# Modulation units of the latent attention layers in halves, spread over query tiles and gates

## The chip, the cores and the metric

The kernel runs as one program on one core of a Trainium2 chip. The metric is the device time of one execution in microseconds (us). All engine times below come from one profiled execution.

## The reference, cut to what matters

Four trunk layers run one after the other on 512 latent tokens and 256 context tokens, both 1024 wide. Layers 0 and 3 mix tokens with latent attention, layer 1 with a windowed attention, layer 2 with a long convolution. Each layer is modulated by two conditions (one for the latent tokens, one for the context):

```python
mx = cond_x @ w_mod[layer] + b_mod[layer]          # (1, 1024) @ (1024, 3072)
shift_x, scale_x, gate_x = jnp.split(mx[:, None, :], 3, axis=-1)
hx = rmsnorm(x, g_pre[layer]) * (1.0 + scale_x) + shift_x
...
x = x + gate_x * rmsnorm(yx, g_post[layer])
```

So `w_mod` of a layer, 12 MB, is read for two rows of conditions. The shift and scale of a layer are wanted when its input is normed; its gate is wanted when its output is added to the stream. A latent attention layer projects the normed input to a key and value latent with the rotary key (320 columns), a query latent (512 columns) and a gate (1024 columns), and goes on to heads, attention and the output projection.

## The kernel before, in words

**Modulation units.** A unit is 512 of the 3072 columns of one layer's modulation, read as four blocks of 512 KB (`want_mod`). For each block `mod_chunk` issues four narrow matmuls (line 442; each shows as two records in the trace, so a block is 8 records and a unit 32). A unit of shift or scale (`mod_ab_unit`) then copies the finished bank to a buffer `m` (ScalarE, line 455), turns it by four transposes (line 459), and reduces it on VectorE (lines 463 to 469). A gate unit (`mod_g_unit`) copies into a buffer that is held until the end of the layer (line 480) and adds the bias row by a small DMA (line 481). `fill` runs one whole unit through; units wait in the list `fillers`.

**Two streams of weights.** `Stream.take` hands out the next block and asks for later ones: `W` for the layer's own weights, `M` for modulation blocks. All loads go through SyncE's queue (line 211, or 209 for some), in one order. `cap_d` and `look_d` bound how many blocks of a stream are loaded and how far ahead. `W` blocks are split into two parts on ScalarE and VectorE (lines 230 to 237) and leave their buffer then; a modulation block leaves its buffer when its matmuls are done.

**Buffers.** All loaded blocks, `m`, the held gate buffer, the normed tile of a query or key tile (`cn`) and the ring of rotary temporaries come out of one arena of float32 buffers of 1024 words a partition. In a latent attention layer the gate and output tensor `og` takes 6144 words of 13760, so that seven such buffers are left. `slot` gives the free buffer that was freed longest ago, and a load into it has to wait for the last reader of what was there.

**The stage that the change touches** is the first part of `layer_A`. It has three loops: six token tiles of the key and value latent (24 matmuls of 320 columns each), six token tiles of the query latent in layer 0 and four in layer 3 (24 matmuls of 512 columns), and eight gate chunks (24 matmuls of 512 columns, in layer 0 also 24 of 256). Each latent tile is normed: a square on ScalarE (line 704), two small GpSimd operations (358, 359), a scaling on VectorE (707), transposes (710) and a split (341, 342). A gate is finished by ScalarE and VectorE (347, 348). Matmuls of latent tiles stand at lines 577 to 579, those of gates at line 588. Tile results are in two double banks `pb`; gates, transposes and modulation go round four banks `pa`.

**Where the units stand.** In layer 0 there are six units (four of shift and scale of layer 1, two of the gate of layer 0). A whole unit goes ahead of each of the key and value tiles 3, 4 and 5 and of the query tiles 0, 1 and 2. In layer 3 there are two units (its own gate), ahead of the key and value tiles 4 and 5. From the first of these tiles on, `M` may hold two blocks (`MC`).

**Order.** The order of the instructions on each engine is planned while the program is built (`TileContext` with `schedule_with_timeline_sim=True`), from the order of the source and from modelled times. On the chip each engine follows that order. So a unit's matmuls can stand inside the matmuls of another tile.

Of the kernel before, what the change touches and what calls it, by code (L numbers as in the profile page):

```python
# [15 lines left out]
AF = mybir.ActivationFunctionType  # L16
# [4 lines left out]
D = 1024  # L21
# [7 lines left out]
AH = 2  # L29
SU = 2  # L30
WX = {25: (3, 2), 27: (3, 2), 29: (3, 3)}
UKS = (3, 4)
UQ = 0
UC = 0
MC = 2
CH = ((0, 384),)
LS = 2
WD = 3
# [97 lines left out]
class Ring:  # L136
# [6 lines left out]
    def next(self):  # L143
        self.i += 1
        return self.blocks[self.i % len(self.blocks)]
# [125 lines left out]
class Kern:  # L271
# [138 lines left out]
    def want_mod(self, unit):  # L410
        kind, L, c = unit
        w = self.io["w_mod"][L].rearrange("(k p) n -> p k n", p=P)
        if kind == "g":
            c += 4
        for kb in range(4):
            n0, k0 = 512 * c + 256 * (kb // 2), 4 * (kb % 2)
            self.M.want(("mod", L, c, kb), w[:, k0:k0 + 4, n0:n0 + 256], split=False)
# [27 lines left out]
            if kb < 3:  # L445
                yield

    def mod_ab_unit(self, L, c, bank=None):

        nc = self.nc  # L450
        bank = bank or self.a
        ps = bank()
        yield from self.mod_chunk(L, c, ps)
        m = self.fs(512)
        nc.scalar.activation(m.ap, ps, AF.Copy)
        yield
        ps = bank()
        for b in range(4):
            nc.tensor.transpose(ps[:, P * b:P * b + P], m.ap[:, P * b:P * b + P], self.ident)
        m.free()  # L460
        part, k0 = c // 2, 4 * (c % 2)
        r = self.col(8).rearrange("p (b s) -> p b s", b=4)
        nc.vector.tensor_reduce(r, ps.rearrange("p (b j s) -> p b s j", b=4, j=4)[:, :, 0:2, :], axis=AX.X, op=ALU.add)
        bm = self.bmod[:, L, 4 * c:4 * c + 4, None].to_broadcast([P, 4, 2])
        if part == 0:
            nc.vector.tensor_tensor(self.ab[:, L, 1, k0:k0 + 4], r, bm, op=ALU.add)
        else:
            nc.vector.scalar_tensor_tensor(r, r, 1.0, bm, op0=ALU.add, op1=ALU.add)
            nc.vector.tensor_tensor(self.ab[:, L, 0, k0:k0 + 4], r, self.gpre[:, L, k0:k0 + 4, None].to_broadcast([P, 4, 2]),
                                    op=ALU.mult)  # L470

    def mod_g_unit(self, L, c, bank=None):

        nc, io = self.nc, self.io
        ps = (bank or self.a)()
        yield from self.mod_chunk(L, 4 + c, ps)
        if c == 0:
            self.mg[L] = self.fs(D)
        m = self.mg[L].ap[:, 512 * c:512 * c + 512]
        nc.scalar.activation(m, ps, AF.Copy)  # L480
        nc.sync.dma_start(out=m[2:3, :], in_=io["b_mod"][L:L + 1, 2048 + 512 * c:2560 + 512 * c])
        yield

# [12 lines left out]
        m.free()  # L496
        return g

    def unit(self, bank=None):
        kind, L, c = self.fillers.pop(0)  # L500
        return (self.mod_ab_unit if kind == "ab" else self.mod_g_unit)(L, c, bank)

    def fill(self, n=1):
        for _ in range(n):
# [186 lines left out]
    def layer_A(self, L, j, h, ctx_out, last):  # L691
        nc, R, F = self.nc, self.R, self.F
# [8 lines left out]
        def normed(ps, n, dst, t):  # L701

            ssq = self.col()
            nc.scalar.activation(self.trash[:, 0:n], ps, AF.Square, accum_out=ssq)
            self.rstd(ssq, n)
            cn = self.fs(n)
            nc.vector.tensor_scalar(cn.ap, ps, ssq, None, op0=ALU.mult)
            pt = self.a()
            for k in range(n // P):
                nc.tensor.transpose(pt[:, P * k:P * k + P], cn.ap[:, P * k:P * k + P], self.ident)  # L710
            cn.free()
            self.split_ps(dst[:, 0, :, P * t:P * t + P], dst[:, 1, :, P * t:P * t + P],
                          pt[:, 0:n].rearrange("p (k n) -> p k n", n=P))

        UK = UKS[0 if ctx_out else 1]
        units = sum(f[:2] in (("ab", L + 1), ("g", L)) for f in self.fillers)

        wide = Banks(self.halves())
        ckv = self.rl(2 * 2 * T)
# [6 lines left out]
        self.W.pump(4, 3)  # L726
        wk = lambda k: (ws[k // 2][1][0][:, k % 2], ws[k // 2][1][1][:, k % 2])
        for t in order:
            if t == UK:
                self.M.cap_d = self.M.look_d = MC  # L730
            if units and t >= UK:
                self.fill()
                units -= 1
            ps = wide.next()
            self.mm_tok(ps[:, 0:320], h, t, wk, 320)
            normed(ps[:, 0:256], 256, ckvv, t)
            ks = small.next()
            kv4 = ks.v(2, 2, 64)
            if t < 4:
                kf = self.ropes.next()  # L740
                self.rope_ps(kf.v(1, 64), ps[:, 256:320].rearrange("p (a b) -> p a b", a=1), t, 1)
                src = kf.ap[:, 0:64]
            else:
                kf = None
                src = ps[:, 256:320]
            nc.scalar.activation(kv4[:, 0], src[:, None, :].to_broadcast([P, 2, 64]), AF.Copy)
            nc.vector.tensor_tensor(kv4[:, 1], src[:, None, :].to_broadcast([P, 2, 64]), kv4[:, 0].bitcast(F32), op=ALU.subtract)
            pt = self.a()
            for i in range(2):
                nc.tensor.transpose(pt[:, P * i:P * i + P], ks.ap[:, P * i:P * i + P].bitcast(F32), self.ident)  # L750
            nc.vector.tensor_copy(krv[:, :, P * t:P * t + P], pt[:, 0:256].rearrange("p (a b) -> p a b", a=2))
# [4 lines left out]
        cqv = cq.v(2, 4, TQ)  # L756
        ws = [self.W.take(("cq", k)) for k in range(0, KD, 2)]
        for t in (order if ctx_out else qt):
            if units and t >= UQ:
                self.fill()  # L760
                units -= 1
            ps = wide.next()
            self.mm_tok(ps, h, t, wk, 512)
            normed(ps, 512, cqv, t)
# [2 lines left out]

        spans = [(0, NX), (NX, NC)] if ctx_out else [(0, NX)]
        for c in range(8):
            if units and c >= UC:  # L770
                self.fill()
                units -= 1
            blk, (wh, wl) = self.W.take(("gate", c))
            outs = [self.a()[:, 0:n] for _, n in spans]
            self.mm_ch(outs, lambda part, k, i: self.h_at(h, part, k, *spans[i]), lambda k: (wh[:, k], wl[:, k]))
            blk.free()
            for (t0, n), o in zip(spans, outs):
                self.gate2(ogv[:, c, t0:t0 + n], o)
        for b in h:
            b.free()  # L780
        self.lo_pool = True
        self.M.cap_d = self.M.look_d = 1

# [152 lines left out]
        units = [(hd, t) for hd in range(8) for t in qt]  # L936
# [861 lines left out]
```

## Time and profile before

| What | Value |
|---|---|
| median of 3 runs | 1950.54 us (1945.15 to 1960.34) |
| time of the profiled execution | 1953.32 us |
| span of its instructions | 1951.5 us |
| granted TensorE clock, mean | 0.984 of full speed |
| TensorE (PE) busy | 1820.0 us, 93% of the span |
| VectorE (DVE), ScalarE (ACT), GpSimd (POOL) busy | 1182.5, 812.3, 521.6 us |

PE is the matmul unit and PEld its weight loads, which lie beside matmuls. SPq is SyncE's queue, which issues DMAs. In a table of stretches the clock is given as a part of full speed; 0.50 is 1.2 GHz and 1.00 is 2.4 GHz. The profiled execution is 2.8 us above the median of the runs.

### The profile page before, as it was taken

The numbers are of one execution on the slowest core, as the hardware profiler recorded it, in microseconds if no ns is written. First come the engines' busy times: TensorE is split into PE (matmuls) and PEld (weight loads), VectorE is DVE, ScalarE is ACT, GpSimd is POOL, SyncE is SP. The second block draws the span as 40 slices with busy tenths as digits, with TensorE's granted clock in tenths as the row PEclk, the third lists the DMA queues.
The fourth block names the chain that finished last, engine by engine and source line by source line (L and its number), as shares of the span: only waits on it lengthen the run. The fifth ranks groups of instructions, "written<-read, shape, count | busy, mean of one in ns | idle before, by whom it ended". The sixth has DMA issues, their size and how long they took to land.

```text
span 1951.5 us, 30304 instructions
## 1 busy us (share of the span) xinstructions
PE 1820.0 (93%) x11628; PEld 1576.6 (81%) x11628; DVE 1182.5 (61%) x2364; ACT 812.3 (42%) x1686; POOL 521.6 (27%) x523
## 2 busy tenths in 40 slices
PE   5879799999999899999989899999998998999998
PEld 3557588999988888888868699999987777889986
DVE  6684134787755367676675445566668553477663
ACT  3473132555544255565664422222222343354451
POOL 5561000000213321221231344444445221000120
PEclk9999899999999999999999999999999999999999
DMA  7857521001133112222362622222221335310121
GB/s 214 259 175 226 158 78 31 22 24 43 44 109 117 57 48 83 76 67 67 99 223 103 204 60 85 70 74 76 76 77 60 122 120 154 87 33 23 44 76 54
DMA packets 186356, 186.31 MB, mean 95 GB/s; under 512 B 16600, under 2 KB 164952, under 8 KB 186212
## 3 DMA queue, kind: packets, MB, share of 16 engines
q1 hardware_dynamic: 186212, 184.39, 30.6%
q8 instruction: 91, 1.49, 0.3%
q14 instruction: 53, 0.43, 0.1%
HBM read 160.24 MB, written 24.12 MB: 94 GB/s over the span
## 4 chain that ended last, share of the span: by engine, by line
PE 77%; DVE 10%; DMA 6%; ACT 3%; issue 3%; POOL 1%; SPq 0%; POOLq 0%; DVEq 0%; ACTq 0%
PE pb L588 13%; PE pb L622 11%; PE pa L588 10%; PE pb L873 5%; PE pa L912 4%; PE pa L1068 3%; PE pa L1049 3%; DMA arena_f<-in_w_mod_dram 3%; PE pa L1525 2%; PE pa L1558 2%; PE pa L442 2%; PE pa L898 2%; PE pa L1177 2%; PE pb L577 2%; PE pb L578 2%
## 5 line engine op out<-in xcount | busy, mean ns | idle before, releaser
L588 PE MATMUL pb<-arena_r 128*128 128x512 f32 (+1 forms) x1536 | 293.2, 345 | 8.1 <-DVE arena_f L1498 3.6
L588 PEld LDWEIGHTS pb<-arena_r 128*128 128x128 f32 x1536 | 239.3, 192 | 40.7 <-issue 3.8
L341 ACT ACTIVATE arena_r<-pa 128x384 fp32r<-128x384 f32 (+2 forms) x382 | 175.3, 478 | 198.5 <-PE pa L898 68.2
L342 DVE TENSOR_TENSOR arena_r<-pa,arena_r 128x384 fp32r<-128x384 f32 (+2 forms) x382 | 199.7, 537 | 86.6 <-ACT arena_r L341 84.9
L588 PE MATMUL pa<-arena_r,swing_R 128*128 128x512 f32 (+1 forms) x816 | 165.9, 355 | 0.6 <-DVE arena_r L342 0.4
L588 PEld LDWEIGHTS pa<-arena_r,swing_R 128*128 128x128 f32 x816 | 132.2, 188 | 21.8 <-DVE arena_r L342 0.6
L873 PE MATMUL pb<-arena_r 128*128 128x384 f32 (+1 forms) x720 | 141.4, 337 | 3.0 <-ACT arena_r L341 1.8
L233 POOL TENSOR_TENSOR swing_R<-arena_f,swing_R 128x1024 fp32r<-128x1024 f32 (+1 forms) x33 | 77.1, 2340 | 200.5 <-ACT swing_R L230 150.7
L873 PEld LDWEIGHTS pb<-arena_r 128*128 128x128 f32 x720 | 119.0, 188 | 5.1 <-ACT arena_r L341 2.5
L668 POOL TENSOR_TENSOR arena_f<-arena_f 128x128 f32<-128x128 f32 (+1 forms) x44 | 20.9, 474 | 364.1 <-DVE small L881 180.1
L622 PE MATMUL pb<-arena_r 128*128 128x512 f32 x480 | 115.2, 393 | 0.0
L358 POOL TENSOR_SCALAR small<-small 128x1 f32<-128x1 f32 x68 | 17.8, 262 | 349.1 <-ACT trash L564 135.6
L622 PEld LDWEIGHTS pb<-arena_r 128*128 128x128 f32 x480 | 89.5, 188 | 20.0 <-issue 1.1
L233 POOL TENSOR_TENSOR arena_r<-swing_F,arena_r 128x1024 fp32r<-128x1024 f32 x34 | 84.6, 2492 | 76.0 <-ACT arena_r L230 73.9
L912 PE MATMUL pa<-arena_r 128*128 128x256 f32 x624 | 91.4, 286 | 2.1 <-DVE arena_r L342 2.1
L912 PEld LDWEIGHTS pa<-arena_r 128*128 128x128 f32 x624 | 81.7, 190 | 4.8 <-ACT arena_r L341 2.5
L1068 PE MATMUL pa<-swing_R,arena_r 128*128 128x256 f32 x576 | 80.2, 289 | 5.1 <-DVE arena_f L348 3.8
L877 DVE TENSOR_REDUCE small<-pb 128x1 f32<-128x768 f32 (+1 forms) x80 | 67.5, 846 | 21.6 <-PE pb L873 20.7
L880 ACT ACTIVATE arena_f<-pb,small 128x768 f32<-128x768 f32 (+1 forms) x80 | 65.2, 816 | 32.9 <-DVE small L878 26.5
L1068 PEld LDWEIGHTS pa<-swing_R,arena_r 128*128 128x128 f32 x576 | 72.9, 192 | 7.3 <-DVE arena_f L348 5.2
L442 PE MATMUL pa<-arena_f,cst 128*32 128x256 f32 x744 | 57.0, 407 | 23.3 <-DMA arena_f<-in_w_mod_dram 23.0
L230 ACT ACTIVATE arena_r<-swing_F 128x1024 fp32r<-128x1024 f32 x34 | 36.2, 1063 | 101.5 <-PE pb L588 93.7
(266 smaller groups left out, 4239.6 us busy)
## 6 DMA issues: line engine op xcount, KB each, us to landing
arena_f<-in_w_mod_dram SPq DMA_DIRECT2D x93, 512.0 KB, 4.8
swing_F<-in_c_w_in_dram SPq DMA_DIRECT2D x31, 512.0 KB, 4.1
kd<-arena_f SPq DMA_DIRECT2D x48, 256.0 KB, 3.4
arena_f<-in_a_w_in_dram SPq DMA_DIRECT2D x24, 512.0 KB, 4.2
arena_f<-kd SPq DMA_DIRECT2D x16, 768.0 KB, 4.5
arena_f<-in_b_w_in_dram SPq DMA_DIRECT2D x20, 512.0 KB, 4.2
x<-arena_f SPq DMA_DIRECT2D x18, 512.0 KB, 4.1
arena_f<-in_a_w_out_dram SPq DMA_DIRECT2D x16, 512.0 KB
```

What stands on the lines that cost most here:

```text
L233: eng.tensor_tensor(lo, view, hi.bitcast(F32), op=ALU.subtract)
L341: self.nc.scalar.activation(hi, src, AF.Copy)
L342: self.nc.vector.tensor_tensor(lo, src, hi.bitcast(F32), op=ALU.subtract)
L442: nc.tensor.matmul(ps[32 * j:32 * j + 32, n0:n0 + 256], self.cst[:, 4 * kh + j, :], w[:, j, :], start=(kh == 0), stop=(kh == 1), skip_grou ...
L588: nc.tensor.matmul(out, l, rhs(part, k, i), start=(k == 0 and q == 0), stop=(k == kt - 1 and q == 2))
L622: nc.tensor.matmul(ys[:, 512 * hf:512 * hf + 512], ov[:, part, k], wt[:, 0, 512 * hf:512 * hf + 512], start=(k == 0 and q == 0), stop=(k = ...
L873: nc.tensor.matmul(S[:, 512 * b:512 * b + w], l, r[:, k0 + w * b:k0 + w * b + w], start=(q == 0), stop=(q == 4))
L877: nc.vector.tensor_reduce(mx, Sv, axis=AX.XY, op=ALU.max)
L880: nc.scalar.activation(pr.v(nb, w), Sv, AF.Exp, bias=mx, scale=sc, accum_out=sm)
L912: nc.tensor.matmul(o[:, 0:256], vv[:, a_, kt % 3, P * hh:P * hh + P], ptv[i // nh][:, b_, i % nh], start=(i == 0 and q == 0), stop=(i == n ...
L1049: nc.tensor.matmul(o, l[:, k], self.h_at(h, part, k, t0, n), start=(k == 0 and i == 0), stop=(k == KD - 1 and i == 2))
L1068: nc.tensor.matmul(ps[:, 0:256], self.h_at(h, part, k, P * t, P), w, start=(k == 0 and i == 0), stop=(k == KD - 1 and i == 2))
```

## The change: halves, and where they stand

`mod_half` computes one half of a unit, 256 columns from two blocks, into a bank of its own, and copies it to its half of the buffer at once. With `halves=True` a unit of shift or scale takes its buffer `m` at the start, runs one half, yields, runs the second, yields, and runs its transposes and the VectorE part when it is called again. A gate unit does the same without transposes. In `layer_A` the units are chained to one generator, `modulate`. It is stepped once ahead of each query tile and once ahead of each gate chunk; no unit stands in the key and value loop. Layer 0 has twelve halves: six ahead of the query tiles 0 to 5, six ahead of the gates 0 to 5. Layer 3 has four, ahead of its four query tiles. `M` may hold two blocks from key and value tile 4 on (and asks for them there), and one from gate 4 on. The units in other layers stay whole.

```diff
+    def mod_half(self, L, c, half, out):
+        nc = self.nc
+        ps = self.a()
+        for kh in range(2):
+            blk, w = self.M.take(("mod", L, c, 2 * half + kh))
+            for j in range(4):
+                nc.tensor.matmul(ps[32 * j:32 * j + 32, 0:256], self.cst[:, 4 * kh + j, :], w[:, j, :], start=(kh == 0), stop=(kh == 1),
+                                 skip_group_check=True)
+            blk.free()
+        nc.scalar.activation(out[:, 256 * half:256 * half + 256], ps[:, 0:256], AF.Copy)
...
+        if halves:
+            m = self.fs(512)
+            for half in range(2):
+                self.mod_half(L, c, half, m.ap)
+                yield
...
+        if halves:
+            if c == 0:
+                self.mg[L] = self.fs(D)
+            m = self.mg[L].ap[:, 512 * c:512 * c + 512]
+            for half in range(2):
+                self.mod_half(L, 4 + c, half, m)
+                if half == 0:
+                    yield
...
-        UK = UKS[0 if ctx_out else 1]
         units = sum(f[:2] in (("ab", L + 1), ("g", L)) for f in self.fillers)
+        def modulate():
+            for _ in range(units):
+                yield from self.unit(halves=True)
+        mods = modulate()
...
         for t in order:
-            if t == UK:
-                self.M.cap_d = self.M.look_d = MC
-            if units and t >= UK:
-                self.fill()
-                units -= 1
+            if t == 4:
+                self.M.cap_d = self.M.look_d = 2
+                self.M.pump()
...
         for t in (order if ctx_out else qt):
-            if units and t >= UQ:
-                self.fill()
-                units -= 1
+            next(mods, None)
             ps = wide.next()
...
         for c in range(8):
-            if units and c >= UC:
-                self.fill()
-                units -= 1
+            if c == 4:
+                self.M.cap_d = self.M.look_d = 1
+            next(mods, None)
             blk, (wh, wl) = self.W.take(("gate", c))
...
+        for _ in mods:
+            pass
```

## Rows read from the trace of the kernel before

**Rows 1.** The page: PE's busy time, the chain by engine, modulation's matmuls.
```profile
PE 1820.0 (93%) x11628; PEld 1576.6 (81%) x11628; DVE 1182.5 (61%) x2364; ACT 812.3 (42%) x1686; POOL 521.6 (27%) x523
...
PE 77%; DVE 10%; DMA 6%; ACT 3%; issue 3%; POOL 1%; SPq 0%; POOLq 0%; DVEq 0%; ACTq 0%
...
L442 PE MATMUL pa<-arena_f,cst 128*32 128x256 f32 x744 | 57.0, 407 | 23.3 <-DMA arena_f<-in_w_mod_dram 23.0
```

**Rows 2.** Stretches of layer 0's stage: length, busy times (instructions), clock, DMA share, GB/s.
```profile
150.00:176.00 26.00, 24.44 (x174) 20.91 (x172) 14.29 (x30) 11.33 (x26) 5.53 (x16) 1.00 0.70 221
...
193.00:209.00 16.00, 7.77 (x48) 5.34 (x44) 4.00 (x8) 2.99 (x5) 0.08 (x1) 0.86 0.89 256
209.00:216.00 7.00, 7.00 (x45) 4.28 (x46) 1.44 (x2) 1.19 (x2) 0.00 (x0) 0.58 0.42 134
216.00:239.60 23.60, 21.73 (x142) 14.37 (x141) 3.41 (x7) 3.76 (x8) 1.48 (x4) 1.00 0.43 139
239.60:313.00 73.40, 73.40 (x420) 64.30 (x419) 22.89 (x35) 20.34 (x38) 2.67 (x6) 1.00 0.22 58
```

**Rows 3.** PE's waits from 150 to 260: total, times, longest.
```profile
PE pa L442 <- DMA arena_f<-in_w_mod_dram: 8.3, 3, 6.8
PE pa L710 <- DVE arena_f L707: 2.0, 3, 1.2
PE pa L459 <- ACT arena_f L455: 1.4, 1, 1.4
```

**Rows 4.** PE in order of time: start, length, instruction, idle before.
```profile
201.49 0.66 PE L459 MATMUL pa<-ident,arena_f 128*128 128x128 f32 x4 [1.40 <-ACT arena_f L455]
208.98 3.64 PE L442 MATMUL pa<-arena_f,cst 128*32 128x256 f32 x32 [6.83 <-DMA arena_f<-in_w_mod_dram]
...
222.91 1.07 PE L442 MATMUL pa<-arena_f,cst 128*32 128x256 f32 x16 [1.08 <-DMA arena_f<-in_w_mod_dram]
...
1621.29 1.94 PE L442 MATMUL pa<-arena_f,cst 128*32 128x256 f32 x32 [0.39 <-DMA arena_f<-in_w_mod_dram]
```

**Rows 5.** Waits of SyncE's queue from 150 to 250, the two longest.
```profile
SPq L211 <- PE pa L442: 21.1, 10, 8.1
SPq L211 <- PE pa L459: 12.5, 3, 5.3
```

**Rows 6.** DMA from 150 to 250: all of it; blocks of modulation (last number: us to landing).
```profile
DMA packets 21665, 18.72 MB, mean 187 GB/s; under 512 B 594, under 2 KB 20658, under 8 KB 21657
...
arena_f<-in_w_mod_dram SPq DMA_DIRECT2D x24, 512.0 KB, 5.1
```

**Rows 7.** Layer 0's gates: matmuls of the first one; what finishes gates, ns min/median/max.
```profile
239.59 5.62 PE L588 MATMUL pa<-arena_r 128*128 128x512 f32 x24
...
251.45 3.04 PE L588 MATMUL pa<-arena_r 128*128 128x256 f32 x24
...
L347 ACT ACTIVATE arena_f<-pa x14: 363/480/599, 245.2 to 305.6; 128x512 f32<-128x512 f32 x7, 128x256 f32<-128x256 f32 x7
...
L348 DVE SCALAR_TENSOR_TENSOR arena_f<-arena_f,pa x14: 414/548/689, 245.9 to 306.3; 128x512 f32<-128x512 f32 x7, 128x256 f32<-128x256 f32 x7
```

**Rows 8.** ScalarE's copy of a whole unit; a copy of 256 columns.
```profile
L455 ACT ACTIVATE arena_f<-pa x16: 578/597/600, 37.9 to 996.6; 128x512 f32<-128x512 f32 x16
...
161.51 0.37 ACT L341 ACTIVATE arena_r<-pa 128x256 fp32r<-128x256 f32 x1
```

**Rows 9.** Layer 3: PE's waits from 1590 to 1660, then two stretches.
```profile
PE pa L710 <- DVE arena_f L707: 2.9, 2, 2.1
...
PE pa L750 <- ACT arena_r L746: 1.6, 1, 1.6
...
PE pa L442 <- DMA arena_f<-in_w_mod_dram: 0.4, 1, 0.4
...
1621.00:1634.00 13.00, 12.71 (x115) 9.90 (x116) 4.44 (x11) 3.48 (x10) 1.91 (x6) 1.00 0.60 187
1634.00:1651.70 17.70, 15.30 (x63) 12.12 (x62) 7.22 (x10) 6.12 (x13) 2.21 (x6) 0.90 0.58 147
```

More of the change, by code (lines that the diff above doesn't have):

```diff
@@ L31 @@
 WX = {25: (3, 2), 27: (3, 2), 29: (3, 3)}
[L32 to L35, printed above, removed]
 CH = ((0, 384),)
@@ L446, in mod_chunk, with mod_ab_unit @@
                 yield
-    def mod_ab_unit(self, L, c, bank=None):
+    def mod_half(self, L, c, half, out):
[8 more added lines that the diff above has]
+        nc.scalar.activation(out[:, 256 * half:256 * half + 256], ps[:, 0:256], AF.Copy)
+    def mod_ab_unit(self, L, c, bank=None, halves=False):
         nc = self.nc
         bank = bank or self.a
[L452 to L456, printed above, removed]
+        if halves:
[3 more added lines that the diff above has]
+                yield
+        else:
+            ps = bank()
+            yield from self.mod_chunk(L, c, ps)
+            m = self.fs(512)
+            nc.scalar.activation(m.ap, ps, AF.Copy)
+            yield
         ps = bank()
@@ L470, in mod_ab_unit, with mod_g_unit @@
                                     op=ALU.mult)
-    def mod_g_unit(self, L, c, bank=None):
+    def mod_g_unit(self, L, c, bank=None, halves=False):
         nc, io = self.nc, self.io
[L475 to L480, printed above, removed]
+        if halves:
[5 more added lines that the diff above has]
+                if half == 0:
+                    yield
+        else:
+            ps = (bank or self.a)()
+            yield from self.mod_chunk(L, 4 + c, ps)
+            if c == 0:
+                self.mg[L] = self.fs(D)
+            m = self.mg[L].ap[:, 512 * c:512 * c + 512]
+            nc.scalar.activation(m, ps, AF.Copy)
         nc.sync.dma_start(out=m[2:3, :], in_=io["b_mod"][L:L + 1, 2048 + 512 * c:2560 + 512 * c])
@@ L497, in gates_out, with unit @@
         return g
-    def unit(self, bank=None):
+    def unit(self, bank=None, halves=False):
         kind, L, c = self.fillers.pop(0)
-        return (self.mod_ab_unit if kind == "ab" else self.mod_g_unit)(L, c, bank)
+        return (self.mod_ab_unit if kind == "ab" else self.mod_g_unit)(L, c, bank, halves)
     def fill(self, n=1):
```

## The prediction, made before the changed kernel was run

> **What bounds the kernel now.** I read the page first. PE is busy 93% of the span and carries 77% of the chain that ended last [rows 1], so a gain has to be time in which PE stands still or runs at the lower clock. The modulation matmuls stand out: 57.0 us busy, and 23.0 us of waiting for their own blocks. Which of that lies where the change acts I took from a table of stretches. In layer 0 the stage runs from 150 to 313. PE is busy 7.77 of 16 us between 193 and 209, while the DMA engines are at 0.89 of their time; it then runs 7 us at a mean clock of 0.58; from 239.6 to 313, in the gates, it is busy all the time and DMA at 0.22 [rows 2]. So the stage has a crowded middle and an empty end for transfers. Third came the waits: 8.3 us for modulation blocks, 2.0 us for normed tiles, 1.4 us for the copy ahead of the transposes [rows 3]. Fourth, PE in order of time: the long wait is one of 6.83 us ahead of a whole unit, whose 32 records then take 3.64 us; the same 32 take 1.94 us at full clock [rows 4]. The waits of SyncE's queue say why a block is late: it stood 21.1 us for buffers that modulation matmuls still read and 12.5 us for those that the transposes of a unit read [rows 5]. The block is asked for late, into a crowd: 24 blocks took a median of 5.1 us to land [rows 6].
>
> **The change part by part.** PE's work stays: as many matmuls of line 442 and as many transposes. A half is 16 records, 1.07 us [rows 4].
>
> *Layer 0, what goes.* Six units had to be fed inside three key and value tiles and three query tiles; now twelve halves stand ahead of six query tiles and six gates. A query tile is 24 matmuls of 512 columns, as many as the first part of a gate, about 5.5 us [rows 7]; a gate has 24 more of 256 columns and is 8.5 us. Two blocks, 1.05 MB, per 5.5 + 1.07 us are 160 GB/s, and per gate 110 GB/s, with its own 0.52 MB 165 GB/s. Both are under the 256 GB/s that the crowded stretch moved [rows 2]. So I take away the 8.3 us of waits for blocks. The 1.4 us for the copy go too: the transposes come a step later, behind a tile of 5.5 us. With the long wait goes the lower clock behind it: (1 - 0.58) x 7.0 = 2.9 us [rows 2]. Together **-12.6 us**. Bounds: -12.6, and 0 if the blocks are as late as before.
>
> *Layer 0, what comes.* (a) Behind a query tile PE has to cover the norm before the transposes of line 710. Now a half of 1.07 us does it where a unit of 1.94 us did; 0.9 us less on six tiles is 0 to 5.2 us. The three such waits were 2.0 us in all [rows 3] although units stood there, and the next tile's matmuls also cover: I take 1.5. (b) Key and value tiles 3 to 5 lose their units as cover. The stretch that holds the tiles without them has 26.00 - 24.44 = 1.6 us of idle PE [rows 2]; 0 to 1.6, I take 0.6. (c) Eight more copies on ScalarE, each unit two of 0.37 instead of one of 0.60 us [rows 8], eight units in both layers: 1.1 us on an engine that is 42% busy, at nothing; if a copy came late, a tile of 5.5 us stands between it and its transposes. (d) In the gates the halves go round the same four banks as the gate results: a gate takes two, a half one, a unit's transposes one more. I counted the turn: only gate 2 finds both its banks just left by gate 1. It then waits for lines 347 and 348, 0.60 + 0.69 us [rows 7], behind 0.66 us of transposes and a half of 1.07 us. So 0, with 1.3 us as the upper bound. (e) Buffers: `m` is now held over two steps, where it was held for one copy. Of seven buffers `W` has two waiting, the rotary ring one, `m` one; three are left for modulation blocks and `cn`. A block for the next step but one then goes into the buffer of the last half or of the last but one `cn`; a step of the query loop is 6.6 us, and the norm ahead of the transposes that free `cn` outlasts a unit's 1.94 us in places [rows 3], so a load starts by estimate 4 us or more before its use. Nothing taken; bound under the first rival. (f) Cutting: 16 records in one piece take 1.07 us, 32 take 1.94 [rows 4], so a unit in two pieces costs 0.2 us more, 1.6 us for eight units; but units stand in pieces of 16 and less already, so 0, with +1.6 as the bound. Layer 0 in sum: -12.6 + 1.5 + 0.6 = **-10.5 us**.
>
> *Layer 3.* Two units leave the key and value tiles 4 and 5, four halves go ahead of its query tiles. The units' blocks were hardly waited for, 0.4 us [rows 9], so this wait is worth nothing. But behind the second unit PE lacked cover: waits of 0.8 us (part of the 2.9 at line 710) and 1.6 us at line 750, and then (1 - 0.90) x 17.7 = 1.8 us at the lower clock [rows 9]. A half now stands there. Bounds: -4.2 us, and +4.3 us if each of the four halves waits as long as the middle one of layer 0's three waits for blocks, 1.08 us [rows 4]. I take **-1 us**, nearer to nothing, because the chain there also runs through the inputs' norms, which the change leaves alone.
>
> Sum: -11.5 us. The profiled execution took 1953.3, so 1941.8 by its own time; it stands 2.8 us above the median of the runs, by which the same sum is 1939.0. I forecast **1940 us**.
>
> **One rule weighed.** Between 193 and 209 the DMA engines are at 0.89 of their time and move 256 GB/s [rows 2]. The Trainium skill, "DMA: Bandwidth & Descriptors", Specifications, gives about 358 GB/s as the limit of HBM for one core; by that limit the crowd is not one of bytes, what holds a block back is its buffer, and a change that spreads bytes and holds `m` longer gains nothing in the wait. By that rule the sum would lose its largest term and come out near no change, which is the first rival. The trace agrees in part: it has the waits for buffers [rows 5], but also engines that are nearly full.
>
> **The rivals.**
> 1. *The waits form again, in small pieces.* Blocks are still tied to buffers, and the planner, which follows modelled times, may put a half ahead of its block as it put a whole unit ahead at 208.98. For it: 33.6 us of the queue's waits are for buffers of units [rows 5], landing takes 5.1 us [rows 6] and the lead in the query tiles may be only the 4 us of (e), so 1.1 us can be missing at each of the ten halves that stand there. Price +11, which takes up the gain: 1951, and up to 1956 with the bounds of (a) and (b). Against it: two blocks a tile where four were wanted. Chance 0.2. That the planner sets two halves together again, so that the change does not do what it says, gives the same time and is counted here.
> 2. *Slower: the tail in gates 4 and 5.* There `M` may hold one block only, so the last three blocks are asked for when they are taken. SyncE's queue is one line; if a weight load in front waits for a buffer, PE stands before line 442 with the load not yet issued. Price: 3 x 5.1 = 15.3 us plus one loss of clock of 2.9, so +18: 1960. It decides when a block's load starts less than its landing time before its place; below that a gate of 8.5 us covers it. For it: the waits of that queue [rows 5]. Against: DMA at 0.22 in the gates, where nothing waited [rows 2]. Chance 0.1.
> 3. *More than forecast.* The waits of line 710 in layer 0 and all 4.2 us in layer 3 go as well, and (a) and (b) come to nothing: -12.6 - 2.0 - 4.2 = -18.8, about 1933. Chance 0.1.
>
> **How the numbers follow.** The forecast has 0.6, with 1932 to 1949 as its own range: at one end 12.6 + 4.2 + 1.6 = 18.4 us under the median (layer 3's bound, and (f) as a gain), at the other 12.6 - 5.2 - 1.6 - 1.3 = 4.5 us under the profiled execution ((a), (b) and (d) at their bounds, layer 3 at nothing). The range that holds eight in ten takes in rival 1 and most of rival 3 and leaves out rival 2: 1929 to 1956. One per cent of the median is 19.5 us, about what a measurement of this kernel tells from no change (its runs lie 15 us apart). Less than 1931 needs rival 3 and some luck in the plan of the rest: 0.1. More than 1970 needs rival 2 twice over: 0.05. Within 1%: 0.85.
>
> **What would show it.** In the changed profile line 442 should wait for its blocks less than 2 us in layer 0's stage, no stretch there should fall under a clock of 0.9, the DMA share in the gates should rise from 0.22 to about 0.6 with PE still full, and the stage should end some 10 us earlier. Waits at line 442 spread over many halves show rival 1; a wait of several us between gates 3 and 5 shows rival 2. Wrong altogether would be a stage that ends earlier and a kernel that does not, because the attention that follows waits for weights whose loads now share the gates with modulation.

## The result, and the profile after

| | before | after |
|---|---|---|
| time, median of 16 runs each, us | 1949.97 (1943.92 to 1960.34) | 1964.84 (1957.76 to 1974.02) |
| ratio | | 1.0075, 95% interval 1.0059 to 1.0092 |
| profiled execution, us | 1953.32, span 1951.5 | 1957.76, span 1956.0 |
| granted clock of the profiled execution | 0.984 | 0.988 |

The change made the kernel **slower by 14.9 us**, 0.75%. The forecast was 1940, faster by 10. Both the number and the direction were wrong.

The two profiles differ by 4.4 us only, and the clock says why. Span times mean granted clock is about the span that would be left at full clock (an estimate: it takes PE for busy where the clock was low). It is 1951.5 x 0.984 = 1920.3 before and 1956.0 x 0.988 = 1932.5 after. So by this estimate the changed kernel has 12.2 us more work and waiting on its path, and its profiled run lost 7.7 us less to the low clock. Over all its runs after has 1931.5 on average, and lost 31.8 us to the clock; its profiled run lost 23.5. The trace of after is therefore good for finding the work and the waits, and flatters the total. All kernels below are given in both ways, as time and as "full clock".

PE's work is the same, as forecast: busy time and count agree with [rows 1]. The halves now stand at line 451, what is left whole at line 438. Together they wait 2.9 + 15.7 = 18.6 us for blocks, where the old line waited 23.0. First the page of after, PE's line; then the groups by line (busy us, mean ns, then idle time before and what ended it).

```profile
PE 1820.0 (93%) x11628; PEld 1575.7 (81%) x11628; DVE 1176.2 (60%) x2364; ACT 813.0 (42%) x1694; POOL 521.9 (27%) x523
```

```profile
L438 PE MATMUL pa<-arena_f,cst 128*32 128x256 f32 x488 | 36.2, 391 | 15.8 <-DMA arena_f<-in_w_mod_dram 15.7
...
L451 PE MATMUL pa<-arena_f,cst 128*32 128x256 f32 x256 | 18.4, 387 | 2.9 <-DMA arena_f<-in_w_mod_dram 2.9
```

**In layer 0 the waits for blocks went, as was said.** The stretches of after that answer to [rows 2], same columns. After reaches this stage at 145.2 us and before at 150.6, so its rows hold work that lies some 5 us further on:

```profile
150.00:176.00 26.00, 22.11 (x128) 20.36 (x127) 14.12 (x34) 10.17 (x27) 6.47 (x18) 0.93 0.45 132
...
193.00:209.00 16.00, 15.39 (x86) 11.20 (x86) 3.15 (x6) 3.05 (x8) 1.48 (x4) 1.00 0.31 100
209.00:216.00 7.00, 7.00 (x47) 5.17 (x43) 0.69 (x1) 1.22 (x3) 0.00 (x0) 1.00 0.47 150
216.00:239.60 23.60, 19.86 (x141) 14.11 (x134) 7.38 (x13) 7.04 (x15) 2.21 (x6) 1.00 0.66 202
239.60:313.00 73.40, 72.96 (x481) 61.07 (x481) 21.97 (x43) 18.92 (x37) 2.92 (x6) 1.00 0.38 108
```

Between 193 and 216 PE is busy 22.39 of 23 us, where it was 14.77; the crowd of 0.89 is 0.31, the clock 0.58 is 1.00. In the gates PE stays full and DMA has risen from 0.22 to 0.38 (0.6 was forecast). But 150 to 176 and 216 to 239.6 now have 3.9 and 3.7 us of idle PE, and 150 to 176 a clock of 0.93. Moved by the 5.4 us these two stretches idle 3.8 and 3.7 us, so the readings do not hang on the shift. PE's waits from 150 to 260, as in [rows 3] (total, times, longest):

```profile
PE pa L733 <- DVE arena_f L730: 6.7, 7, 2.1
PE pa L451 <- DMA arena_f<-in_w_mod_dram: 2.1, 1, 2.1
PE pa L777 <- DVE arena_r L774: 0.9, 1, 0.9
PE pa L473 <- ACT arena_f L454: 0.6, 1, 0.6
```

The waits for blocks fell from 8.3 to 2.1 us and the one for the copy from 1.4 to 0.6. The waits for normed tiles (line 733, once 710) rose from 2.0 to 6.7. Over the whole stage, from its first key and value matmul to attention's first score, PE idles 14.4 us before and 12.8 us after:

```profile
150.63:340.90 190.27, 175.84 (x1112) 144.16 (x1111) 68.22 (x136) 53.69 (x116) 16.49 (x42) 0.96 0.41 122
```

```profile
145.19:332.40 187.21, 174.42 (x1115) 144.32 (x1116) 67.78 (x136) 55.88 (x124) 17.15 (x42) 0.98 0.42 125
```

SyncE's queue, as in [rows 5], from 150 to 250:

```profile
SPq L207 <- PE pa L473: 22.4, 4, 7.5
...
SPq L207 <- PE pa L451: 7.5, 4, 2.8
```

It stands for buffers that modulation reads 7.5 us instead of 21.1, but 22.4 instead of 12.5 for those that a unit's transposes read; `m`, which these read, is held longer.

**The loss is in layer 1, whose source the change does not touch.** The stretch from layer 1's first mixing matmul to its last, before and after (columns as in [rows 2]; these windows and the like ones below have that length and lie 1.5 us late at both ends):

```profile
700.50:1017.90 317.40, 296.61 (x2327) 255.46 (x2326) 228.92 (x593) 189.37 (x493) 81.06 (x91) 0.99 0.32 102
```

```profile
688.00:1016.60 328.60, 299.69 (x2305) 256.43 (x2303) 230.00 (x593) 188.08 (x492) 80.23 (x91) 0.98 0.30 94
```

It is 11.2 us longer, for the same matmuls: 8.1 us more of idle PE (28.9 against 20.8) and 3.1 us more of busy PE, which is lower clock. What SyncE's queue waited for there, before and then after:

```profile
SPq L211 <- DMA arena_f<-in_w_mod_dram: 17.7, 9, 3.0
```

```profile
SPq L207 <- DMA arena_f<-in_w_mod_dram: 35.0, 14, 7.2
```

The queue stands twice as long behind modulation blocks that have not landed yet. These two numbers are the signature by which I read the experiments.

**Where it comes from.** The following is worked out from the kernel's own allocation of its buffers and was then tried. When layer 1 begins, one weight block of its own, loaded ahead in layer 0's output phase, is still held in the float32 arena. The change takes and frees buffers at other places than before, `m` above all is held over two steps, so the turn of free buffers after layer 0 is another (which of these moves it was not separated), and this block lies 4 KB lower in each partition: 5.75 KB are free between layer 1's `og` and the block, where there were 9.75. Before, three blocks of probabilities and two of their sums just fitted in there. Now two fit; the third and the sums go into the part that modulation blocks and weights rotate through, and **three buffers rotate in layer 1 where four did**. As the program's order is planned from modelled times, the whole plan of layer 1 changes with it.

### The profile page after: what moved, and what is told of

Same layout as the page of the kernel before. It is cut to its first block, busy times and chain, and to the rows that moved or that the text cites. A ratio compares the mean times of both kernels' runs of the same rounds, so it can differ in the third digit from the quotient of the medians.

```text
span 1956.0 us, 30330 instructions
## 1 busy us (share of the span) xinstructions
PE 1820.0 (93%) x11628; PEld 1575.7 (81%) x11628; DVE 1176.2 (60%) x2364; ACT 813.0 (42%) x1694; POOL 521.9 (27%) x523
## 5 line engine op out<-in xcount | busy, mean ns | idle before, releaser
L611 PE MATMUL pa<-arena_r,swing_R 128*128 128x512 f32 (+1 forms) x816 | 166.8, 356 | 1.1 <-ACT arena_f L454 0.5
L691 POOL TENSOR_TENSOR arena_f<-arena_f 128x128 f32<-128x128 f32 (+1 forms) x44 | 20.8, 473 | 408.6 <-DVE arena_f L690 223.4
L229 POOL TENSOR_TENSOR swing_R<-arena_f,swing_R 128x1024 fp32r<-128x1024 f32 (+1 forms) x33 | 76.1, 2311 | 187.3 <-ACT swing_R L226 133.1
L354 POOL TENSOR_SCALAR small<-small 128x1 f32<-128x1 f32 x68 | 18.6, 274 | 326.1 <-ACT trash L587 136.6
L904 DVE TENSOR_REDUCE small<-pb 128x1 f32<-128x768 f32 (+1 forms) x80 | 67.5, 846 | 21.6 <-PE pb L900 20.8
L1076 PE MATMUL pa<-arena_r,swing_R 128*128 128x512 f32 (+1 forms) x384 | 73.4, 341 | 1.6 <-DVE arena_r L1102 1.4
```

The costliest lines, as they stand in the source:

```text
L229: eng.tensor_tensor(lo, view, hi.bitcast(F32), op=ALU.subtract)
L611: nc.tensor.matmul(out, l, rhs(part, k, i), start=(k == 0 and q == 0), stop=(k == kt - 1 and q == 2))
L904: nc.vector.tensor_reduce(mx, Sv, axis=AX.XY, op=ALU.max)
L1076: nc.tensor.matmul(o, l[:, k], self.h_at(h, part, k, t0, n), start=(k == 0 and i == 0), stop=(k == KD - 1 and i == 2))
```

## The experiments

"Full clock" is the mean over the runs of span times granted clock, "lost" the mean of what remains of the span. The before that ran beside e1 to e4 had a median of 1950.39 us (its row in the table), the one beside e5 to e8 1950.99 with a full clock of 1918.9, the one beside after 1949.97. Ratios are each to its own before.

| kernel | buffers in layer 1 | median, us | ratio to before, 95% | full clock | lost |
|---|---|---|---|---|---|
| before | 4 | 1950.4 | | 1918.8 | 30.3 |
| after | 3 | 1964.8 | 1.0075, 1.0059 to 1.0092 | 1931.5 | 31.8 |
| e1: after, four buffers | 4 | 1949.2 | 0.9979, 0.9965 to 0.9994 | 1918.8 | 26.9 |
| e2: before, three buffers | 3 | 1969.7 | 1.0095, 1.0074 to 1.0116 | 1931.2 | 36.4 |
| e3: before, turned, four | 4 | 1952.5 | 1.0012, 0.9999 to 1.0026 | 1919.2 | 31.5 |
| e4: e1, layer 3 whole | 4 | 1943.3 | 0.9962, 0.9947 to 0.9977 | 1915.5 | 26.4 |
| e5: before, banks turned | 4 | 1948.0 | 0.9983, 0.9973 to 0.9994 | 1918.4 | 27.8 |
| e6: before, one buffer kept | 3 | 1966.4 | 1.0071, 1.0053 to 1.0089 | 1929.9 | 33.7 |
| e7: before, layer 3 in halves | 4 | 1957.2 | 1.0021, 1.0010 to 1.0032 | 1924.7 | 29.0 |
| e8: e4, halves at gates only | 4 | 1955.7 | 1.0018, 1.0007 to 1.0028 | 1922.6 | 30.3 |

Three full-clock values lie at 1929.9 to 1931.5: they are the three kernels with three buffers. The others lie at 1915.5 to 1924.7.

The second table has lengths of stretches, from landmarks in each profile (us): layer 0's stage from its first key and value matmul to attention's first score; its output phase up to layer 1's first mixing matmul; layer 1 from the first to the last of these; the last column runs from the end of layer 2's convolution through its output phase and layer 3's stage to layer 3's first score.

| kernel | layer 0's stage | output phase | layer 1 | up to layer 3's score |
|---|---|---|---|---|
| before | 190.3 | 159.8 | 317.4 | 215.1 |
| after | 187.2 | 156.5 | 328.6 | 218.8 |
| e1 | 186.8 | 156.5 | 315.7 | 216.5 |
| e2 | 189.1 | 159.8 | 329.4 | 216.4 |
| e3 | 187.3 | 160.4 | 322.8 | 216.8 |
| e4 | 189.6 | 156.8 | 315.5 | 216.6 |
| e5 | 192.9 | 157.0 | 315.7 | 215.7 |
| e6 | 190.7 | 160.3 | 329.4 | 215.6 |
| e7 | 190.3 | 159.7 | 317.3 | 220.9 |
| e8 | 199.3 | 156.6 | 319.5 | 215.6 |

### e1, e2, e3: turn the buffers by hand

A buffer is taken and freed at once at the start of layer 0's output phase. No instruction is added; only the turn in which buffers are handed out moves. One such step gives the changed kernel its fourth buffer back (e1); two steps take it from the kernel before (e2); one step leaves the kernel before with four (e3, the control).

```diff
+TURN = {0: 1}          # e1 and e3; {0: 2} in e2
...
     def w_out_phase(...)
+        for _ in range(TURN.get(L, 0)):
+            self.fs(1024).free()
```

> The changed kernel, with one float32 buffer taken and given back (no instruction) where layer 0's output phase begins. This turns the order in which buffers are handed out by one, so that the weight block that is held when layer 1 begins lies higher, its rings of probabilities and sums fit beneath it, and layer 1 keeps four rotating buffers as in the kernel before, not three as in the changed kernel. Theory (buffers): the 9 to 12 us won by the start of layer 1's background work stay, the 8 us lost inside layer 1 and most of the 6 us lost around its end go: 1938 us (1933 to 1944), ratio 0.991 to 0.997. Rival (any new plan): layer 1's order on the engines is worse because it was planned anew, whatever the buffers: 1955 to 1968. Rival (halves cost by themselves later): 1960 to 1968.

> The kernel before, with two buffers taken and given back one after the other at the same place: the held block lies lower, a ring of layer 1 has to be laid into the rotating part, and layer 1 is left with three rotating buffers, as in the changed kernel. Units stay whole, in their old places. Theory (buffers): layer 0 unchanged, 8 us lost from the first modulation block of layer 1 to its end and some 6 us after it: 1963 us (1957 to 1969), ratio 1.004 to 1.010. Rival (any new plan): 1946 to 1954 or any other value, with no longer waits for modulation blocks in layer 1. Rival (halves cost by themselves later): 1950.

> The kernel before, with one buffer taken and given back at the same place: the held block lies at the same place as in the first of these kernels, layer 1 has four rotating buffers in another turn. Control for the turn itself. Theory (buffers): 1950 us (1946 to 1954), no change. Rival (any new plan): a change of 5 us or more either way, since the buffers and so the plan of layer 1 differ.

Measured: 1949.2, 1969.7 and 1952.5 us. e3 lies in its range. e2 is 0.7 us above the range of the buffers (its ratio of 1.0095 is in it). e1 is 5 us above the range of the buffers and below those of both rivals: the loss in layer 1 went as expected, but the lead of 9 to 12 us that the expectation kept from one pair of profiles was mostly not the change's (see the part on why). With four buffers the whole loss of the change is gone and a little more; without any change, three buffers cost 18.5 us. The control is 0.12% off, with an interval that reaches 0.9999. Layer 1 in e1 and then in e2:

```profile
687.80:1003.50 315.70, 296.54 (x2327) 255.49 (x2325) 229.56 (x594) 189.04 (x493) 80.75 (x91) 0.99 0.33 103
```

```profile
693.70:1023.10 329.40, 300.16 (x2304) 255.92 (x2302) 231.35 (x593) 187.90 (x492) 80.47 (x91) 0.98 0.30 95
```

And the signature, the queue's waits for landing modulation blocks, in e1 and then in e2:

```profile
SPq L210 <- DMA arena_f<-in_w_mod_dram: 18.4, 9, 2.9
```

```profile
SPq L214 <- DMA arena_f<-in_w_mod_dram: 33.7, 13, 5.4
```

e1 has before's value and e2 has after's, the reverse of what their sources would say. e3 shows a limit of single profiles: its layer 1 is 322.8 us long with four buffers, but it fell to the low clock for 13.7 us there, where before fell for 3.4, and over all runs its full-clock time is before's.

### e6: is it the number of buffers?

e2 moves the turn in everything that follows as well. So e6 takes a buffer away in layer 1 alone, and gives it back at its end.

```diff
         small = Ring(self, "rl", 512, 1)
+        kept = self.fs(1024)
...
+        kept.free()
```

> The kernel before, with one of layer 1's four rotating buffers taken at the start of the layer and kept to its end; layer 0, the placing of all long-lived rings, and the buffers of layers 2 and 3 stay as before. If the number of buffers is the cause: 11 to 13 us more between layer 1's first mixing matmul and its last (317 to 323 before), SyncE's queue waits some 34 us for landing modulation blocks there instead of 18, and 1966 us (1960 to 1972) in all. If it is the other placing of rings or the state that layers 2 and 3 take over: 1950 us (1946 to 1954).

Measured: 1966.4 us, 1.0071. Layer 1's stretch and then the signature in e6:

```profile
695.30:1024.60 329.30, 302.15 (x2308) 257.80 (x2307) 229.97 (x594) 187.55 (x494) 80.96 (x91) 0.98 0.29 92
```

```profile
SPq L211 <- DMA arena_f<-in_w_mod_dram: 35.0, 13, 5.5
```

That is after's layer 1 (328.60 and 35.0) in a kernel that has no halves at all, and all of it as expected. The number of buffers is shown to be the cause of layer 1's loss. By full clock the fourth buffer is worth 11.0 (e6), 12.4 (e2) and 12.7 us (after against e1); by the ratios 13.9, 18.5 and 18.7, since kernels with three buffers also run at the lower clock for longer. What e2 and after lose beyond e6, which takes the buffer in layer 1 alone, is not traced to a place.

### e5: 3 us that came from a bank

In every kernel that has the halves in layer 0 the output phase is 3 us shorter, though nothing of the change stands there. The halves leave the turn of the PSUM banks at another place. e5 moves this turn in the kernel before, without any instruction.

```diff
     def w_out_phase(...)
+        if L == 0:
+            self.ia += 2
```

> The kernel before, whole units, with one change of numbering and no instruction: the turn of the four banks pa is moved on by two where layer 0's output phase begins, as the six extra banks of layer 0's halves move it (six is two in a turn of four). Theory (banks): the 3.2 us that the kernels with halves win between the start of layer 0's output phase and layer 1's first mixing matmul (156.5 instead of 159.8 us) come from this alone, because layer 1 gives fixed banks to its loops and the last norms of layer 0 no longer use the first of them: that stretch 156 to 157.5 us, the whole 1947 us (1943 to 1950). Rival: they come from the halves or from the plan: 159 to 161 us in that stretch, 1950 us in all.

Measured: 1948.0 us, 0.9983, and 157.0 us for the stretch, both as expected. So the saving is shown to be the turn of banks. The end of the stretch in before and then in e5:

```profile
600.00:650.00 50.00, 44.92 (x309) 40.70 (x308) 30.04 (x47) 19.36 (x34) 24.28 (x32) 1.00 0.26 83
650.00:699.02 49.02, 45.51 (x343) 42.90 (x341) 15.24 (x36) 13.21 (x27) 11.41 (x13) 0.97 0.16 49
```

```profile
598.14:648.14 50.00, 46.08 (x320) 42.05 (x319) 30.27 (x47) 19.55 (x35) 25.41 (x33) 1.00 0.28 88
648.14:694.40 46.26, 42.74 (x332) 40.07 (x331) 15.33 (x36) 12.99 (x27) 10.77 (x11) 1.00 0.15 46
```

PE idles 7.4 us instead of 8.6 in these two pieces, and its clock stays at 1.00 where it fell to 0.97 (0.03 x 49 = 1.5 us). Over all runs most of the 3.0 us is clock: by full clock e5 gains 0.5 us on its own before (1918.4 for 1918.9) and loses 3.0 us less to the low clock (27.8 for 30.7). Layer 1 starts on fixed banks, and the last norms of layer 0 no longer hold them; this sentence is read from the code, the runs show only that the turn does it.

### e4 and e7: layer 3

e4 is e1 with layer 3's two units whole again, ahead of key and value tiles 4 and 5. e7 is the kernel before with halves in layer 3 only: it has the change's `mod_half` and its branches for halves, and steps them ahead of each query tile and gate.

```diff
 # e4, in layer_A
-        mods = modulate()
+        mods = modulate() if ctx_out else iter(())
...
             if t == 4:
                 self.M.cap_d = self.M.look_d = 2
-                self.M.pump()
+                if ctx_out:
+                    self.M.pump()
+            if not ctx_out and t >= 4 and units:
+                self.fill()
+                units -= 1
```

```diff
 # e7, in layer_A of before
+        mods = iter(())
+        if not ctx_out:
+            mods = (0 for _ in range(units) for _ in self.unit(halves=True))
+            units = 0
...
                 self.M.cap_d = self.M.look_d = MC
+                if not ctx_out:
+                    self.M.pump()
...
+            next(mods, None)
```

> As the first of these kernels, but layer 3's two units stay whole, ahead of its key and value tiles 4 and 5, as before. Theory: the gain is all layer 0's, layer 3 is worth 0 to 1 us, so within 2 us of the first kernel: 1938 us (1933 to 1945). My forecast had 1 us for layer 3. A rival in which layer 3's halves cost several us would give a time 3 us or more below the first kernel.

> The kernel before, with halves in layer 3 alone (ahead of its query tiles); layers 0 to 2 stay. The difference between the first and the fourth kernel that ran here (1949.2 with and 1943.3 us without) says that they cost 3 to 6 us: 1954 us (1952 to 1957). My forecast was a gain of 1 us: 1949. No difference would be 1949 to 1952, and would leave the difference between those two kernels to chance.

Measured: e4 1943.3 us, 0.9962, **faster than both kernels**; e7 1957.2 us, 1.0021. So e4 is 3.3 us (by the ratios) to 5.9 us (by the medians) below e1, not within 2 us of it: its rival held. e7 is 0.2 us above its range and far from my forecast's 1949. Halves in layer 3 cost 3.3 us by the ratios of e1 and e4, 4.1 by that of e7, and 3.3 and 5.8 by full clock. PE's waits in e7's layer 3 stage, to be held beside [rows 9]:

```profile
PE pa L737 <- DVE arena_f L734: 4.7, 3, 2.1
...
PE pa L455 <- DMA arena_f<-in_w_mod_dram: 1.4, 1, 1.4
...
PE pb L605 <- POOL swing_R L233: 0.7, 1, 0.7
```

The wait for normed tiles is 4.7 us for 2.9, that for blocks 1.4 for 0.4; the 1.6 us at line 750 are gone, as forecast. In all PE idles 16.4 us in e7's stretch where it idled 13.7, and is busy 3.0 us longer for the same matmuls, in part at the lower clock. So the halves lengthen the waits for normed tiles that they were to cover. e1 and e4 show the same in idle time (14.8 and 13.0 us), though their stretches are equally long (216.5 and 216.6): e4's profile has more of the low clock there.

### e8: do the query tiles need the halves as cover?

e8 is e4 with layer 0's twelve halves two by two ahead of the gates 0 to 5, none at a query tile.

```diff
         for t in (order if ctx_out else qt):
-            next(mods, None)
...
         for c in range(8):
             next(mods, None)
+            next(mods, None)
```

> Layer 0's twelve halves go two by two ahead of the gates 0 to 5, none ahead of a query tile; layer 3 whole, layer 1 with four rotating buffers. It tests the norm's cover: in the changed kernel PE waited 6.7 us for normed query tiles in layer 0's stage, where I had 1.5 us more than before. If a half is the cover that counts, these waits grow by about one half's 1.07 us at each of five tiles, to 10 to 13 us, and the kernel is 2 to 6 us slower than the one with halves ahead of queries and gates (1943.3): 1947 us (1944 to 1951). If the waits come from the planned order whatever stands there, they stay at 5 to 8 us and the time at 1943 (1939 to 1946), as gates had no wait in them before.

Measured: 1955.7 us, 12.4 above e4 (10.9 by the ratios), and above the ranges of both expectations. PE's waits in layer 0's stage, e4 first and e8 second:

```profile
PE pa L738 <- DVE arena_f L735: 7.7, 7, 3.0
...
PE pa L454 <- DMA arena_f<-in_w_mod_dram: 1.9, 1, 1.9
```

```profile
PE pa L738 <- DVE arena_f L735: 9.1, 6, 4.1
PE pa L454 <- DMA arena_f<-in_w_mod_dram: 6.0, 4, 2.0
```

The norm waits rose by 1.4 us only, between the two expectations, so how much a half covers is not settled by it. What it does show: two halves together at a gate bring back block waits of 6.0 us for 1.9, and the stage is 9.7 us longer, 7.4 of it idle PE. In these two kernels the transfers follow one half at a place and not two.

## Why the prediction was wrong

**The step that failed is (e), buffers: "Nothing taken; bound under the first rival."** I counted the buffers of layer 0 and asked whether a load there would come too late. I did not ask what the arena looks like when layer 0 is over. The change's other takes and frees, among them the longer hold of `m`, move the turn of buffers, with it the place of one block, and with that the fourth buffer of layer 1: +17.5 us of mean time between e1 and after (12.7 of work and waits, 4.9 of clock, each rounded), more than any term of the sum. The bound could not hold it, since it was taken from rows between 150 and 250. The same gap stands under "What would show it": I looked for a loss in the attention that follows, whose heads took 198.3 us before and 197.5 after, and no further.

**Layer 0, -10.5 forecast, about -3 measured.** The waits that were to go went, but others came, so the mechanism was right and its size was not. The stage is 190.3, 187.3, 192.9, 190.7, 190.3 and 189.1 us long in the six kernels with whole units (mean 190.1), and 187.2, 186.8 and 189.6 in the three with halves at tiles and gates (mean 187.9): -2.2, and -0.8 in the heads. The lengths of the two groups overlap; PE's idle time in the stage does not, 14.2 to 15.7 us in the six (mean 14.8) and 12.8 to 13.7 in the three (mean 13.2), so -1.6. e4 says the same another way: -7.1 us against before, less the 3.0 of e5 for the bank, is -4.1. By terms:
- Waits for blocks, -8.3 forecast: -6.2 in the trace. Nearly right; by the limit of the Trainium skill, "DMA: Bandwidth & Descriptors", Specifications, which the prediction weighed, they should have stayed. The trace goes against that reading: PE's waits for blocks and the crowd of 0.89 went, although the queue's waits for buffers of units stayed, 29.9 us for 33.6, and those for buffers of normed tiles rose from 11.2 to 31.9.
- Copy, -1.4: -0.8.
- Low clock, -2.9: the 10.24 us piece at half clock (from 204.6) is gone. PE was busy for 6.1 us of it, so it cost some 3.0, as forecast. But after has pieces of 3.41 us at 160.6 and 184.5, in which PE is busy nearly throughout: up to 3.4 us. So about nothing between 150 and 313; before has one more such piece at 327.5, which makes some -1.7 over the whole stage.
- (a) Cover of the norm, +1.5 with a bound of 5.2: +4.7 (2.0 to 6.7). This is the mis-sized term. I took it low because "the next tile's matmuls also cover"; here they did not cover enough.
- (b) +0.6: 150 to 176 idles 3.9 us where it idled 1.6, so +2.3, beyond the bound of 1.6, though part of it is of the norms under (a).

**What looked like the forecast in the trace.** At the end of layer 0's stage after stands 8.5 us ahead of before (attention's first score at 332.4 for 340.9), close to the 10 us I had forecast. Most of it was not the change: before reached the stage at 150.6, after at 145.2, the others at 144.6 to 148.4 without regard to halves. Ahead of the stage before's profiled run was at half clock for 13.6 us and after's for 6.8, which is 3.4 of these 5.4 us; the other 2 are not traced. Without the other kernels' lengths I should have believed it.

**Layer 3, -1 forecast: +3 to +6** (e7, e1 against e4). The sign taken was wrong; the bound of +4.3 was for waits for blocks, and what grew most were those for normed tiles. The cover that PE lacked behind the second unit came at the price of cover at the tiles that lost it.

**(d), banks, 0 to +1.3 within the gates:** there it was right, PE is busy 72.96 of 73.40 us. But the turn of banks has a worth outside of them, -3.0 us (e5, most of it clock), which I did not look for.

**The rivals.** Rival 1 (waits for blocks again, in small pieces) fell: one such wait of 2.1 us is left in the stage. What took up two thirds of that gain were the waits for normed tiles, which stand under (a). Rival 2 gave the right direction for a wrong reason: in the gates of after PE idles 0.4 us in all. Rival 3 fell.

In sum: -3 to -4 (layer 0), -3.0 (bank), +3 to +4 (layer 3), +17.5 (buffer) make +13.5 to +15.5, for 14.9 measured. This agreement is weak evidence: -4.1, -3.0, e1 against e4 and after against e1 are steps of one chain of kernels and must add up. What stands apart from it are the stage lengths for layer 0, e7 for layer 3, and e2 and e6 for the buffer. Not settled is why layer 1 with three buffers also meets the lower clock more: after lost 4.9 us more to it than e1 and e2 6.1 more than before, while e6 lost 3.0 more, and no run was made that separates it from the idle time that goes with it.

## What to carry to other kernels

An edit that changes how long a buffer is held, or how many banks are taken, reaches every later layer that draws from the same pool: before pricing it, lay out the pool at the entry of each later stage, before and after, and look for a block that no longer fits. Pin such a layout (here a buffer taken and freed at once, with no instruction) and time the change again, because a gain (the change with its fourth buffer back is at -0.2% in e1, and without layer 3's halves at -0.4% in e4, with the bank's 3.0 us in both) can be buried under a change that nobody made. And compare a stage by its own length in several kernels, with the granted clock taken out, not by where it ends in one profile.

## What was not expected of the hardware

The low clock is a part of every time here: 26 to 36 us of 1950, estimated as span times (1 - granted clock), and up to 18 us apart between runs of one kernel (0.979 to 0.988 in after, so 0.009 x 1960). With it taken out, the kernels with whole units and four buffers agree within 0.8 us: before 1918.8 and 1918.9, e3 1919.2, e5 1918.4, where their medians lie between 1948.0 and 1952.5. (e1 is at 1918.8 too, but there a gain in layer 0 and a loss in layer 3 cancel.) Of two kernels that differ by less than 1%, the mean granted clock of each should be read before the time.
